# Fused layer-norm pieces, four weight slots and a routing-first passage to the experts, in a two-layer streaming step

## The chip, the cores and the metric

One core of a Trainium2 chip runs the whole program. The metric is the device time of one execution in microseconds (us): the kernel before takes 1603.79 us, the median of three runs (1601.14 to 1604.37). Engines are named as in the profile: PE is the matrix engine (TensorE), DVE is VectorE, ACT is ScalarE, POOL is GpSimd, and SP is the queue that issues most transfers (DMAs).

## The reference

288 tokens (256 of a prompt, 32 of a decode step) of width 1024 pass through two layers. In each layer:

```
z = x @ W_in                       # queries, keys, values, latents and two gates
m = W_out( sigmoid(ga) * Woa(FoX(x)) + sigmoid(gb) * Wob(MLA(x)) )
h = LN(alpha * x + m)
y = LN(alpha * h + FFN(h) + sigmoid(h W_pg) * (p W_pp))
```

FoX and MLA are two attention mixers. FFN is a dense SwiGLU of width 2816 in layer 0, and in layer 1 a mixture: a router picks the best 2 of 8 experts for each token, and each expert is a SwiGLU of width 2816. Everything is float32; besides y the new cache rows are returned.

## The kernel before, in words

**Layout.** Activations lie feature-major: 8 pieces of 128 features by 288 tokens. Weights come from memory in chunks of 128 x 1024 float32 (512 KB), each eight 128 x 128 tiles. Every product is made of three float32r matmuls: ACT copies a weight chunk, rounded, to `wh` (the high part) and `wl = raw - wh` (the low part) is subtracted on DVE and POOL; activations are split likewise into `xh` and `xl`. Lines 242 to 244 issue the three: xh·wh, xl·wh, xh·wl. The halves `wh` and `wl` have three slots of 1024 columns, given out in turn (`weight_slot`); a slot is free when the last matmul that reads it has run.

**Stages.** For each layer: "in" products and attention, gates and output products, a first layer norm (LN1), the feed-forward part, a second layer norm (LN2, in layer 0 inside the program, in layer 1 at its end). During LN1 PE has the eight small "pp" products (6 matmuls each; L643 moves each result from PSUM to `ple`), and behind them the eight "pg" products (24 matmuls each). These need all eight normalised pieces, since each piece is one step of the contraction. During LN2 of layer 0 PE has nothing but the "in" products of layer 1, which need the same; two of them end in a copy out of PSUM by DVE (`cq`, L402) that frees their PSUM buffers.

**A layer norm** (`norm_apply`, line 563). Two matmuls give mean `pm` and mean square `pv` over the features. ACT makes m2 (L597) and a copy mu (L598), DVE the variance (L599, L600), ACT the square root (L602), DVE the reciprocal (L608). Then a loop over the pieces c: DVE and POOL subtract mu (L577; piece 0 on DVE, the others on POOL), DVE multiplies by rstd (L616), ACT makes xh with gain and bias (L617), DVE (c < 5) or POOL makes x (L626), and DVE makes xl = x - xh (L629). Weight chunks of the products behind are split in between. All of it stands in a `manual_schedule` block, in which DVE, ACT and POOL keep the order that is written. PE, and everything outside such blocks, is ordered by the framework's planner from its own estimates. Each engine then runs its list strictly in that order.

**From LN1 of layer 1 to the experts** (the passage, L1266 to L1274). Three pg products, then the router (`route`: 24 small "lgp" matmuls, some forty small DVE operations, two "posp" matmuls), then `tokens` (transposes of x, copies to `xt` by DVE and ACT, three stores to a buffer `xd` in memory, L835), then slot lists (`slots`: one-hot matrices `dm` by DVE, L916, and "gsp" matmuls), then `fetch` (POOL gathers an expert's 128 token rows from `xd`, L928), then the remaining pg products, and `gather` (PE transposes the gathered rows, "gp", L939). The first expert product is "gu".

**Experts.** Eight experts in turn, each 66 half chunks of weights streamed through a ring (`mraw`) of 1 MB buffers, some 24 half chunks ahead; each half is split by ACT (L894), DVE (832 columns) and POOL (192, L896). "dn" is the product of an expert's second matrix.

## Time and profile before

| | before |
|---|---|
| median of three runs (lowest, highest) | 1603.79 us (1601.14, 1604.37) |
| the profiled execution, its time | 1602.14 us |
| the profiled execution, its span | 1600.4 us |
| PE / DVE / ACT / POOL busy | 95% / 74% / 62% / 53% |
| mean granted TensorE clock | 0.98 of full speed |

Times inside the trace are counted from the first instruction; the profiled execution's own time is 1.7 us longer than its span. A row of a timeline gives start, duration and, in brackets, how long the engine stood idle ahead of it and who ended that wait.

### The profile page before, as it was taken

How to read it: one execution, taken by the hardware profiler on the slowest of the kernel's cores; microseconds unless marked ns; L12 is line 12 of the kernel's file. 1: busy time of each engine (PE TensorE's matmuls, PEld its weight loads, DVE VectorE, ACT ScalarE, POOL GpSimd, SP SyncE). 2: the span in 40 equal slices, each digit the busy share in tenths (PEclk: the TensorE clock that was granted, in tenths of full speed). 3: DMA queues.
4: the chain of work that ended last, by engine and by line, in shares of the span. 5: the costliest groups of instructions: out<-in, count | busy, mean ns of one | idle time of the engine just before them, and what ended most of it. 6: DMA issues, size and time to landing. Idle time of an engine off the chain costs nothing. (4 is left out here: it accounts for less than half of the span.)

```text
span 1600.4 us, 25001 instructions
## 1 busy us (share of the span) xinstructions
PE 1526.9 (95%) x8930; PEld 1353.7 (85%) x8930; DVE 1178.0 (74%) x1567; ACT 993.1 (62%) x1417; POOL 850.3 (53%) x735
## 2 busy tenths in 40 slices
PE   6999998999997999998699999999999999999995
PEld 6999998999996999997587878878788787787874
DVE  6654667554458664578688888888888898888887
ACT  5454455444344464444487787877878778787784
POOL 5000132000016000245498887988879888898997
PEclk9999999999998999998899999999999999999998
DMA  7523444555553523883689999999999999999950
GB/s 213 181 65 105 154 133 145 163 167 163 167 166 111 174 80 93 275 298 106 235 333 361 351 362 350 361 360 343 372 347 366 357 352 357 346 360 347 349 188 32
DMA packets 85540, 391.61 MB, mean 245 GB/s; under 512 B 9728, under 2 KB 11648, under 8 KB 63776
## 3 DMA queue, kind: packets, MB, share of 16 engines
q1 hardware_dynamic: 83120, 382.76, 67.9%
q0 software_dynamic: 2224, 7.13, 1.4%
q8 instruction: 72, 1.18, 0.3%
q14 instruction: 60, 0.49, 0.1%
q10 hardware_dynamic: 64, 0.05, 0.0%
HBM read 384.75 MB, written 5.11 MB: 244 GB/s over the span
## 5 line engine op out<-in xcount | busy, mean ns | idle before, releaser
L896 POOL TENSOR_TENSOR wl<-mraw,wh 128x192 fp32r<-128x192 f32 x530 | 674.8, 1293 | 111.2 <-ACT wh L894 101.0
L896 DVE TENSOR_TENSOR wl<-mraw,wh 128x832 fp32r<-128x832 f32 x530 | 587.3, 1116 | 104.1 <-ACT wh L894 98.9
L894 ACT ACTIVATE wh<-mraw 128x1024 fp32r<-128x1024 f32 x530 | 556.3, 1057 | 133.3 <-PE dn L244 45.3
L227 DVE TENSOR_TENSOR wl<-raw,wh 128x1024 fp32r<-128x1024 f32 (+1 forms) x193 | 236.5, 1227 | 165.0 <-ACT wh L217 164.8
L217 ACT ACTIVATE wh<-raw 128x1024 fp32r<-128x1024 f32 (+1 forms) x196 | 199.3, 1020 | 241.5 <-PE mm L243 122.9
L242 PE MATMUL mm<-xh,wh 128*128 128x288 f32 x992 | 301.2, 305 | 22.3 <-DVE cq L402 7.7
L243 PE MATMUL mm<-xl,wh 128*128 128x288 f32 x992 | 301.6, 305 | 7.2 <-DVE xl L629 7.0
L244 PE MATMUL mm<-xh,wl 128*128 128x288 f32 x992 | 299.8, 303 | 0.3 <-DVE wl L227 0.2
L242 PE MATMUL gu<-wh,xg 128*128 128x512 f32 x704 | 283.2, 403 | 0.0
L243 PE MATMUL gu<-wl,xg 128*128 128x512 f32 x704 | 281.3, 400 | 1.0 <-DVE wl L896 0.9
L244 PE MATMUL gu<-wh,xg 128*128 128x512 f32 x704 | 277.9, 395 | 0.0
L242 PEld LDWEIGHTS mm<-xh,wh 128*128 128x128 f32 x992 | 192.4, 195 | 25.0 <-ACT xh L263 6.6
L243 PEld LDWEIGHTS mm<-xl,wh 128*128 128x128 f32 x992 | 191.3, 193 | 9.5 <-DVE xl L629 8.3
L244 PEld LDWEIGHTS mm<-xh,wl 128*128 128x128 f32 x992 | 191.2, 193 | 1.4 <-DVE wl L227 0.8
L243 PEld LDWEIGHTS gu<-wl,xg 128*128 128x128 f32 x704 | 132.8, 189 | 29.5 <-DVE wl L896 2.2
L242 PEld LDWEIGHTS gu<-wh,xg 128*128 128x128 f32 x704 | 132.5, 188 | 29.8 <-ACT xg L263 0.2
L244 PEld LDWEIGHTS gu<-wh,xg 128*128 128x128 f32 x704 | 132.3, 188 | 28.8 <-DVE xg L264 0.2
L243 PE MATMUL dn<-wl,hb 128*128 128x512 f32 (+1 forms) x374 | 144.3, 386 | 6.3 <-DVE wl L896 4.2
L244 PE MATMUL dn<-wh,hb 128*128 128x512 f32 (+1 forms) x374 | 142.6, 382 | 0.0
L242 PE MATMUL dn<-wh,hb 128*128 128x512 f32 (+1 forms) x374 | 142.6, 382 | 0.0
L550 POOL COPY s<-r 128x288 f32<-128x288 f32 x3 | 1.3, 425 | 178.4 <-DVE r L738 169.7
L243 PEld LDWEIGHTS dn<-wl,hb 128*128 128x128 f32 x374 | 70.2, 188 | 24.3 <-DVE wl L896 7.6
(343 smaller groups left out, 2142.2 us busy)
## 6 DMA issues: line engine op xcount, KB each, us to landing
mraw<-we SPq DMA_DIRECT2D x169, 1024.0 KB, 6.4
mraw<-we SPq DMA_DIRECT2D x192, 512.0 KB, 6.1
raw<-ws SPq DMA_DIRECT2D x187, 512.0 KB, 3.6
ok<-ka SPq DMA_DIRECT2D x2, 576.0 KB, 5.3
ov<-vf SPq DMA_DIRECT2D x4, 256.0 KB
xd<-xt SPq DMA_DIRECT2D x2, 512.0 KB, 3.2
x<-xT SPq DMA_DIRECT2D x3, 288.0 KB, 5.9
y<-ple SPq DMA_DIRECT2D x3, 288.0 KB, 2.1
```

Of the source, the lines that this page charges most:

```text
L217: self.nc.scalar.activation(wh[:, c:c + w], raw[:, c:c + w], AF.Copy)
L227: eng.tensor_tensor(wl[:, s], raw[:, s], wh[:, s].bitcast(F32), op=ALU.subtract)
L242: nc.tensor.matmul(ps, w[0], x[0], start=start, stop=False)
L243: nc.tensor.matmul(ps, w[0], x[1], start=False, stop=False)
L244: nc.tensor.matmul(ps, w[1], x[0], start=False, stop=stop)
L550: nc.gpsimd.tensor_copy(self.s1, rc)
L894: nc.scalar.activation(wh[:, c:c + w], src[:, c:c + w], AF.Copy)
L896: eng.tensor_tensor(wl[:, s], src[:, s], wh[:, s].bitcast(F32), op=ALU.subtract)
```

## The change

1. `norm_apply` is written anew. Per piece, DVE makes r·g·rstd in one operation (`scalar_tensor_tensor`), ACT adds the bias for xh, DVE makes xl = (t + b) - xh in one operation, and ACT makes x. So x moves from DVE and POOL to ACT. The subtraction of the mean reads `pm` in PSUM on DVE, except pieces 1 and 2, which stay on POOL. One pp product instead of two is evicted ahead of the square root; mu is copied behind it. The weight chunks of the next products are split before and during the norm at other places, by ACT and DVE alone.
2. Four weight slots instead of three. `qa`, `mh`, `ml` and others move into shared buffers.
3. In `linear` the three matmuls stand as xh·wh, xh·wl, xl·wh.
4. The passage is one hand-ordered block: logits and token transposes first, then pg0, routing, slot lists of experts 0 and 1 (index columns alone), their fetches, pg1 to pg7 with the gate values worked out between them. ACT does all `xt` copies and issues the stores to `xd`. The slot lists of experts 2 to 7 move into expert 0.

What moved, in three places. First ACT in LN1 of layer 0, before, from the square root (L602) on; `ple` rows evict pp products, `wh` rows split weight chunks:

```order
L602 ACTIVATE lrstd<-lrstd,eps 128x288 [waits DVE_49]
L604 ACT_TABLE_LOAD
L604 ACTIVATE warm<-mu 128x1 [waits Activation_49]
L643 ACTIVATE ple<-mm 128x288 [waits PE_49]
L217 ACTIVATE wh<-raw 128x1024 [waits DMAHW4_49]
L643 ACTIVATE ple<-mm 128x288 [waits PE_49] x2
L617 ACTIVATE xh<-r,vec 128x288 [waits DMASW2_49,DVE_49]
L643 ACTIVATE ple<-mm 128x288 [waits PE_49]
L217 ACTIVATE wh<-raw 128x1024 [waits DMAHW5_49]
L617 ACTIVATE xh<-r,vec 128x288 [waits DVE_49]
L643 ACTIVATE ple<-mm 128x288 [waits PE_49]
L617 ACTIVATE xh<-r,vec 128x288 [waits DVE_49]
```

and now (square root L610, `xh` L623, `x` L634, chunk splits L219):

```order
L610 ACTIVATE lrstd<-lrstd,eps 128x288 [waits DVE_49]
L611 ACTIVATE mu<-pm 128x288
L613 ACT_TABLE_LOAD
L613 ACTIVATE warm<-mu 128x1 [waits Activation_49]
L648 ACTIVATE ple<-mm 128x288
L648 ACTIVATE ple<-mm 128x288 [waits PE_49] x2
L219 ACTIVATE wh<-raw 128x512 [waits DMAHW7_49,PE_49]
L623 ACTIVATE xh<-r,vec 128x288 [waits DMASW2_49,DVE_49]
L648 ACTIVATE ple<-mm 128x288
L623 ACTIVATE xh<-r,vec 128x288 [waits DVE_49]
L648 ACTIVATE ple<-mm 128x288
L634 ACTIVATE x<-r,vec 128x288
```

One `ple` row fewer stands ahead of the table load, the first half of pg3's chunk, which waits for PE because its slot held pp weights, stands ahead of the first `xh`, and `x` rows have come to ACT.

Second, DVE in the same norm, two pieces of the loop, before:

```order
L616 TENSOR_TENSOR r<-r,lrstd 128x288 [waits Pool_49]
L626 TENSOR_SCALAR x<-r,vec 128x288 [waits DVE_49]
L629 TENSOR_TENSOR xl<-x,xh 128x288 [waits Activation_49]
L616 TENSOR_TENSOR r<-r,lrstd 128x288 [waits Pool_49]
L626 TENSOR_SCALAR x<-r,vec 128x288 [waits DVE_49]
L629 TENSOR_TENSOR xl<-x,xh 128x288 [waits Activation_49]
L227 TENSOR_TENSOR wl<-raw,wh 128x768 [waits DMAHW5_49]
```

and now (L622 is r·g·rstd, L584 the subtraction, L632 `xl`):

```order
L622 SCALAR_TENSOR_TENSOR r<-r,vec,lrstd 128x288 [waits Pool_49]
L584 TENSOR_TENSOR r<-r,pm 128x288
L632 SCALAR_TENSOR_TENSOR xl<-r,vec,xh 128x288 [waits Activation_49]
L622 SCALAR_TENSOR_TENSOR r<-r,vec,lrstd 128x288
L584 TENSOR_TENSOR r<-r,pm 128x288
L229 TENSOR_TENSOR wl<-raw,wh 128x512 [waits Activation_49]
L632 SCALAR_TENSOR_TENSOR xl<-r,vec,xh 128x288 [waits Activation_49]
```

Per piece DVE had three operations and now has three others, of which one is the subtraction that POOL made.

Third, PE around the gather of expert 0's rows, before (the last pg7 matmuls, then "gp", then "gu"):

```order
L243 MATMUL mm<-xl,wh 128x288
L244 MATMUL mm<-xh,wl 128x288
L939 MATMUL gp<-ident,xt 128x128 [waits DMASW4_49]
L939 MATMUL gp<-ident,xt 128x128 x7
L242 MATMUL gu<-wh,xg_7757 128x512 [waits Activation_49]
L243 MATMUL gu<-wl,xg_7757 128x512
L244 MATMUL gu<-wh,xg_7758 128x512 [waits DVE_49]
```

and now, inside pg4 and behind the index columns of expert 1:

```order
L255 MATMUL mm<-xh,wh 128x288
L256 MATMUL mm<-xh,wl 128x288
L257 MATMUL mm<-xl,wh 128x288
L940 MATMUL gsp<-gm,dm 128x2 [waits DVE_49,PE_49]
L940 MATMUL gsp<-gm,dm 128x2 [waits DVE_49] x2
L963 MATMUL gp<-ident,xt 128x128 [waits DMASW4_49,DVE_49,PE_49]
L963 MATMUL gp<-ident,xt 128x128 x3
L256 MATMUL mm<-xh,wl 128x288 [waits DVE_49]
L257 MATMUL mm<-xl,wh 128x288
```

The rows that fetch the gathered tokens stood behind all pg products; half of them now stands in the middle of pg4, and three and a half pg products are left behind it. The other half follows the gate columns, behind pg5:

```order
L256 MATMUL mm<-xh,wl 128x288
L257 MATMUL mm<-xl,wh 128x288
L940 MATMUL gsp<-gm,dm 128x2 [waits DVE_49]
L940 MATMUL gsp<-gm,dm 128x2 x5
L963 MATMUL gp<-ident,xt 128x128 x4
L255 MATMUL mm<-xh,wh 128x288 [waits Activation_49] x2
L256 MATMUL mm<-xh,wl 128x288 [waits DVE_49]
```

The diff:

```diff
     def weight_slot(self):
-        self.slot = (self.slot + 1) % 3
+        self.slot = (self.slot + 1) % 4
         s = slice(1024 * self.slot, 1024 * self.slot + 1024)
         return self.wh[:, s], self.wl[:, s]
 
-    def weight_hi(self, n, parts=1):
+    def weight_raw(self, n):
         raw = self.raw_tile(n % 3 == 2, "raw")
         self.nc.sync.dma_start(raw, self.i["ws"][n])
-        wh, wl = self.weight_slot()
+        return (raw, *self.weight_slot())
...
-        self.chunks = {k: v for k, v in self.chunks.items() if k > n - 3}
+        self.chunks = {k: v for k, v in self.chunks.items() if k > n - 4}
...
-            self.mm3(ps, self.weight(t + k), x, start and k == 0, stop and k == len(xs) - 1)
+            w, x = self.weight(t + k), x
+            nc = self.nc
+            nc.tensor.matmul(ps, w[0], x[0], start=start and k == 0, stop=False)
+            nc.tensor.matmul(ps, w[1], x[0], start=False, stop=False)
+            nc.tensor.matmul(ps, w[0], x[1], start=False, stop=stop and k == len(xs) - 1)
...
-    def norm_apply(self, l, off, r, last, head, ms, after):
+    def norm_apply(self, l, off, r, last, head, ms, mid=None, late=()):
...
-        after = list(after)
+        late = dict(late)
 
...
-        def sub(c, eng):
-            eng.tensor_tensor(r[:, c, :], r[:, c, :], mu, op=ALU.subtract)
-
-        pend = []
-
-        def hi():
-            if after:
-                n = after.pop(0) // CB
-                pend.append((n,) + self.weight_hi(n))
-
-        def lo(cut=CB * P):
-            if pend:
-                self.weight_lo(*pend.pop(0), cut=cut)
+        def sub(c):
+            eng, m = (nc.gpsimd, mu) if c in (1, 2) else (nc.vector, pm)
+            eng.tensor_tensor(r[:, c, :], r[:, c, :], m, op=ALU.subtract)
+
+        def half(c):
+            if mid is not None:
+                s = slice(c, c + 512)
+                nc.scalar.activation(wh[:, s], raw[:, s], AF.Copy)
+                return lambda: nc.vector.tensor_tensor(wl[:, s], raw[:, s], wh[:, s].bitcast(F32), op=ALU.subtract)
+            return lambda: None
 
         with self.tc.manual_schedule(engines={ENG.DVE, ENG.Activation, ENG.Pool}):
             last()
             c = KD - 1
+            if mid is not None:
+                raw, wh, wl = self.weight_raw(mid // CB)
+                self.chunks[mid // CB] = (wh, wl)
+            lo = [half(0)]
...
+            lo.pop()()
             nc.scalar.activation(m2, pm, AF.Square)
-            nc.scalar.activation(mu, pm, AF.Copy)
+            lo = [half(512)]
...
-            fill(2)
+            fill(1)
             nc.scalar.activation(rstd, rstd, AF.Sqrt, bias=self.eps[:, 0:1])
+            nc.scalar.activation(mu, pm, AF.Copy)
             if head is not None:
                 nc.scalar.activation(self.warm, mu[:, 0:1], AF.Tanh)
-            sub(0, nc.vector)
-            sub(1, nc.gpsimd)
-            sub(2, nc.gpsimd)
+            sub(0)
+            for c in (1, 2):
+                sub(c)
             nc.vector.reciprocal(rstd, rstd)
-            fill(1)
-            hi()
-            fill(2)
+            fill(3)
             for c in range(KD + 1):
                 if c < KD:
-                    g, b = self.col(l, off + c), self.col(l, off + 8 + c)
-                    t = r[:, c, :]
-                    nc.vector.tensor_tensor(t, t, rstd, op=ALU.mult)
-                    nc.scalar.activation(self.xh[:, c, :], t, AF.Identity, scale=g, bias=b)
+                    g, b, t = self.col(l, off + c), self.col(l, off + 8 + c), r[:, c, :]
+                    nc.vector.scalar_tensor_tensor(t, t, g, rstd, op0=ALU.mult, op1=ALU.mult)
+                    nc.scalar.activation(self.xh[:, c, :], t, AF.Identity, bias=b)
                     if c == 0:
-                        lo(512)
-                        for z in range(3, KD):
-                            sub(z, nc.gpsimd)
+                        lo.pop()()
                     fill(1)
-                    if c in (0, 4):
-                        hi()
-                    eng = nc.vector if c < 5 else nc.gpsimd
-                    eng.tensor_scalar(self.x[:, c, :], t, g, b, op0=ALU.mult, op1=ALU.add)
+                    if c + 3 < KD:
+                        sub(c + 3)
                 if c:
                     p = c - 1
-                    nc.vector.tensor_tensor(self.xl[p // 4][:, p % 4, :], self.x[:, p, :], self.xh[:, p, :].bitcast(F32), op=ALU.subtract)
-                if c in (3, 6):
-                    lo(768 if c == 3 else 1024)
+                    b, t = self.col(l, off + 8 + p), r[:, p, :]
+                    nc.vector.scalar_tensor_tensor(self.xl[p // 4][:, p % 4, :], t, b, self.xh[:, p, :].bitcast(F32),
+                                                   op0=ALU.add, op1=ALU.subtract)
+                    nc.scalar.activation(self.x[:, p, :], t, AF.Identity, bias=b)
+                if c in late:
+                    self.weight(late[c])
...
-            mg = self.pool(f"mg{l}", stack=sm)
-            mh = mg.tile([P, KD, T], F32R, name="mh")
-            ml = mg.tile([P, KD, T], F32R, name="ml")
+            mh = g.tile([P, KD, T], F32R, tag="A", name="mh")
+            ml = [g.tile([P, 4, T], F32R, tag=t, name="ml") for t in ("B1", "B2")]
...
+            t = [WHERE[(l, "pg"), m] for m in range(4)]
+            self.weight(t[0])
             self.ple = g.tile([P, KD, T], F32, tag="C", name="ple")
-            self.norm_apply(l, 0, r, evict, lambda m: self.pp(l, m), range(8), [WHERE[(l, "pg"), m] for m in range(3)])
+            self.xh = g.tile([P, KD, T], F32R, tag="A", name="xh")
+            self.xl = [g.tile([P, 4, T], F32R, tag=t, name="xl") for t in ("B1", "B2")]
+            self.norm_apply(l, 0, r, evict, lambda m: self.pp(l, m), range(8), t[1], {3: t[2], 7: t[3]} if l % 2 else {3: t[2]})
...
-            self.weight(t[0])
-            self.weight(t[1])
-            self.norm_apply(l, 16, r, evict, None, (), t[2:])
...
+            for x in t:
+                self.weight(x)
+            self.norm_apply(l, 16, r, evict, None, ())
...
+    def logits(self):
+        nc = self.nc
+        t = [self.ps_t.tile([P, 512], F32, tag="t", name="lgp") for z in range(2)]
+        self.lgp = [t[0][:, 0:NE], t[1][:, 0:NE], t[0][0:TS, NE:2 * NE]]
+        for bs in ((0, 1), (2,)):
+            for k in range(KD):
+                for b in bs:
+                    n = TS if b == 2 else P
+                    nc.tensor.matmul(self.lgp[b], self.x[:, k, b * P:b * P + n], self.wr[:, k, :], start=k == 0, stop=k == KD - 1)
+
+    def tokens(self):
+        nc, m1 = self.nc, self.m1
+        self.xd = self.dpool.tile([T, D], F32, name="xd")
+        xt = [m1.tile([P, D], F32, tag="xt", bufs=3, name="xt") for b in range(3)]
+        for z in range(2):
+            for b, n in enumerate((P, P, TS)):
+                pt = self.mps("tp", True)
+                for c in range(4):
+                    nc.tensor.transpose(pt[0:n, c * P:(c + 1) * P], self.x[:, 4 * z + c, b * P:b * P + n], self.ident)
+                nc.scalar.activation(xt[b][0:n, 512 * z:512 * z + 512], pt[0:n], AF.Copy)
+                if z:
+                    nc.scalar.dma_start(self.xd[b * P:b * P + n, :], xt[b][0:n])
+
+    def route(self, between):
...
+        for b in range(3):
+            for z in range(b + 1):
+                nc.tensor.matmul(ps[:, 8 * b:8 * b + 8], self.tri if z == b else self.ones, sel[:, z, :], start=z == 0, stop=z == b)
+        for b in range(3):
+            nc.tensor.matmul(ps[:, 32:40], self.ones, sel[:, b, :], start=b == 0, stop=b == 2)
+        self.cnt = ps[:, 32:40]
+        self.pos = m1.tile([P, 3, NE], F32, name="pos")
+        between()
+        nc.vector.scalar_tensor_tensor(self.pos, ps[:, 0:24].rearrange("p (b e) -> p b e", b=3), 1.0, sel, op0=ALU.add, op1=ALU.mult)
+
+    def gates(self):
...
-            if e + 2 < NE:
+            if 0 < e < NE - 2:
...
-                if e == 0 and g in (2, 5):
-                    self.slots((4, 5) if g == 2 else (6, 7))
+                if e == 0 and g in (1, 4, 7):
+                    self.slots((2 * (g // 3 + 1), 2 * (g // 3 + 1) + 1))
+                    if g == 1:
+                        self.fetch(2)
...
-        self.pgate(1, pgt, range(3), 6)
-        self.route()
-        self.tokens()
-        self.slots((0, 1))
-        self.fetch(0)
-        self.fetch(1)
-        self.cut = 512
-        self.pgate(1, pgt, range(3, 7), 6)
-        self.gather(0)
-        self.slots((2, 3))
-        self.pgate(1, pgt, range(7, 8), 6)
+        self.marks()
+        with self.tc.manual_schedule(engines={ENG.DVE, ENG.Activation, ENG.Pool}):
+            self.logits()
+            self.tokens()
+            ps = self.linear((1, "pg"), 0, self.xs())
+            n = WHERE[(1, "pg"), 4] // CB
+            raw, wh, wl = self.weight_raw(n)
+            self.chunks[n] = (wh, wl)
+            nc.scalar.activation(wh, raw, AF.Copy)
+
+            def low(c):
+                nc.vector.tensor_tensor(wl[:, c:c + 512], raw[:, c:c + 512], wh[:, c:c + 512].bitcast(F32), op=ALU.subtract)
+
+            self.route(lambda: low(0))
+            self.slots((0,), (2, 4))
+            self.fetch(0)
+            low(512)
+            self.slots((1,), (2, 4))
+            self.fetch(1)
+            gate(0, ps=ps)
+            gate(1)
+            self.weight(WHERE[(1, "pg"), 5])
+            gate(2)
+            self.gates()
+            gate(3)
+            self.slots((0, 1), (0, 2))
+            self.weight(WHERE[(1, "pg"), 6])
+            gate(4)
+            self.weight(WHERE[(1, "pg"), 7])
+            self.gather(0)
+            gate(5)
+            gate(6)
+            gate(7)
```

## Rows read from the trace of the kernel before

**Rows 1.** Windows by stage; the heading line names the columns, x the number of instructions

```profile
core 0: us, PE busy (x) PEld busy (x) DVE busy (x) ACT busy (x) POOL busy (x), PEclk, DMA share, GB/s
234.00:258.00 24.00, 17.63 (x102) 16.24 (x100) 20.63 (x32) 14.12 (x26) 12.57 (x12) 0.86 0.22 67
486.00:510.00 24.00, 13.42 (x78) 12.24 (x79) 21.41 (x37) 13.17 (x23) 15.91 (x15) 0.79 0.17 58
719.00:746.00 27.00, 22.05 (x152) 20.49 (x151) 21.67 (x35) 14.89 (x28) 13.89 (x14) 0.87 0.19 59
746.00:785.30 39.30, 24.10 (x168) 23.06 (x166) 28.41 (x85) 10.06 (x18) 20.85 (x23) 0.80 0.67 231
728.95:735.77 6.82, 5.81 (x24) 5.20 (x23) 6.30 (x14) 3.64 (x6) 2.75 (x4) 0.50 0.22 73
747.00:752.00 5.00, 5.00 (x40) 5.00 (x39) 4.75 (x11) 0.12 (x2) 4.74 (x5) 1.00 0.82 236
786.00:1570.00 784.00, 778.64 (x3538) 629.00 (x3537) 677.08 (x806) 617.59 (x737) 675.35 (x528) 1.00 0.91 339
```

**Rows 2.** Waits of TensorE: waiting line <- releaser: us in total, times, longest

```profile
PE gp L939 <- DMA xt<-xd,ati: 12.7, 1, 12.7
PE mm L243 <- DVE xl L629: 7.0, 6, 2.4
PE dn L243 <- DVE wl L896: 4.2, 9, 0.5
PE mm L242 <- ACT ple L643: 4.2, 3, 2.0
```

**Rows 3.** Timeline of VectorE, first layer norm of layer 0: start, us

```profile
233.70 0.46 DVE L599 TENSOR_TENSOR lrstd<-pv,m 128x288 f32<-128x288 f32 x1 [3.92 <-PE pv L596]
243.00 1.05 DVE L616 TENSOR_TENSOR r<-r,lrstd 128x288 f32<-128x288 f32 x1
247.75 0.45 DVE L616 TENSOR_TENSOR r<-r,lrstd 128x288 f32<-128x288 f32 x1
```

**Rows 4.** Timeline of GpSimd, same norm

```profile
240.11 4.60 POOL L577 TENSOR_TENSOR r<-r,mu 128x288 f32<-128x288 f32 x5
```

**Rows 5.** Timeline of ScalarE, same norm

```profile
234.99 0.54 ACT L602 ACTIVATE lrstd<-lrstd,eps 128x288 f32<-128x288 f32 x1 [1.24 <-DVE lrstd L600]
235.54 1.28 ACT L604 ACT_TABLE_LOAD   x1
241.32 0.63 ACT L617 ACTIVATE xh<-r,vec 128x288 fp32r<-128x288 f32 x1 [0.68 <-DVE r L616]
```

**Rows 6.** Timeline of TensorE, second layer norm of layer 0

```profile
493.60 1.09 PE L242 MATMUL mm<-xh,wh 128*128 128x288 f32 x3 [5.99 <-ACT xh L617]
497.11 0.61 PE L243 MATMUL mm<-xl,wh 128*128 128x288 f32 x1 [2.42 <-DVE xl L629]
509.76 0.37 PE L242 MATMUL mm<-xh,wh 128*128 128x288 f32 x1 [1.79 <-DVE cq L402]
```

**Rows 7.** Timeline of VectorE, second layer norm of layer 0

```profile
488.20 0.77 DVE L600 TENSOR_SCALAR lrstd<-lrstd 128x288 f32<-128x288 f32 x1
```

**Rows 8.** Timeline of TensorE, last router matmuls, gather and first expert product

```profile
744.64 1.11 PE L756 MATMUL lgp<-wr,x 128*128 128x8 f32 x20
783.52 1.97 PE L939 MATMUL gp<-ident,xt 128*128 128x128 f32 x8 [12.66 <-DMA xt<-xd,ati]
785.32 0.79 PE L242 MATMUL gu<-wh,xg 128*128 128x512 f32 x1
```

**Rows 9.** Timeline of VectorE, router and slot lists

```profile
750.54 0.18 DVE L766 TENSOR_REDUCE mx<-lg 128x3 f32<-128x24 f32 x1
750.75 0.18 DVE L768 TENSOR_TENSOR sel<-lg,mx 128x24 f32<-128x24 f32 x1
759.65 2.40 DVE L916 TENSOR_SCALAR dm<-iota,pos 128x128 fp32r<-128x128 f32 x6
```

**Rows 10.** The gather of token rows, its own view, all eight

```profile
DMA to landing us min/median/max: 3.9/5.9/9.1
```

More of the change, by code (lines that the diff above doesn't have):

```diff
@@ L67, in plan @@
             + [[(256 * j + 64, 64), (256 * j + 192, 64)] for j in range(4)])
-        lin((l, "gate"), "w_in", l, KD, [c for m in range(8) for c in
-            ([(GAOFF + m * P, P)], [(GBOFF + m * P, P)])])
+        lin((l, "gate"), "w_in", l, KD, runs(GAOFF, 8) + runs(GBOFF, 8))
         for m in range(8):
@@ L695, in phase @@
             r = g.tile([P, KD, T], F32, tag="D", name="r")
-            ms = self.pieces(mh, ml)
+            ms = [(mh[:, k, :], ml[k // 4][:, k % 4, :]) for k in range(KD)]
             self.pp_load(l)
@@ L800, in route @@
+        for b in range(3):
[5 more added lines that the diff above has]
+    def gates(self):
+        nc, m1 = self.nc, self.m1
+        mx1, s1, mx2, s2 = self.tops
         most = m1.tile([P, 1], F32, name="most")
-        nc.vector.tensor_reduce(most, cnt, axis=AX.X, op=ALU.max)
+        nc.vector.tensor_reduce(most, self.cnt, axis=AX.X, op=ALU.max)
```

135 lines of the change are left out of this document (57 added, 78 removed).

## The prediction

> **What bounds the kernel now.** I read the windows by stage first. Over the experts PE is busy 778.64 of 784 us at full clock [rows 1]: that half of the program is PE's, and only the 5.4 us in which it isn't busy can be won there. Around the layer norms and in the passage it is otherwise. From 486 to 510 PE is busy 13.42 of 24 us, and from 719 to the first expert product at 785.3 it is busy 22.05 + 24.10 = 46.15 of 66.3 us, with mean clocks of 0.79, 0.87 and 0.80 [rows 1]. So a change of norms and passage acts on the path, through two things: time in which PE stands, and time at half clock after it has stood (24 matmuls took 5.81 us in one half-clock stretch, 0.24 each, while 40 instructions, some of them short, took 5.00 in a full one [rows 1]; I count 0.13 for a 288-column matmul there). Second, PE's waits say on what: the gather 12.7 us once, `xl` 7.0 in six waits, `ple` 4.2, the experts' `wl` 4.2 in nine [rows 2]; the first `xh` of layer 0's second norm adds 5.99 [rows 6]. Third, the timelines of those places give the durations below.
>
> All sums are against the profiled execution, 1602.14 us, which lies 0.1% under the median of the runs, 1603.79; a difference worked out for the one is used for the other.
>
> **Pace of a piece.** A 128 x 288 operation on DVE takes 0.45 us at 247.75 and 1.05 at 243.00 [rows 3]; the slow one stands in the stretch in which POOL makes five subtractions in 4.60 us [rows 4]. The change takes all but two subtractions from POOL, all its x and all its chunk halves, so I price DVE's three operations of a piece at 3 x 0.45 = 1.35 us. The subtraction now reads PSUM: the row `lrstd<-pv,m` reads PSUM too and takes 0.46 [rows 3], so no surcharge. [...] ACT now has, per piece, xh and x. The old xh with gain and bias took 0.63; the square root, with a bias alone, 0.54 [rows 5]. So 2 x 0.54 = 1.08, plus a pp eviction of some 0.39 in LN1: 1.47 us. In LN1 ACT, not DVE, sets the pace; in LN2 DVE does.
>
> **LN2 of layer 0: -6.3 us.** The chain to the first xh loses the contended halves: 0.3 on the maximum (0.77 [rows 7]), 0.6 on r·rstd (1.05 to 0.45), 0.1 on xh, and some 0.3 because mu no longer stands ahead; PE restarts near 492.3 instead of 493.60 [rows 6]. The wait for the first xl, 2.42 [rows 6], shrinks to about one piece. Eight pieces at 1.35 end near 492 + 10.8 = 502.5 to 503; nine matmuls per piece fit in 1.2 us at full clock and trail in 2.2 at half, so the product ends between 503.5 and 505. With three finished chunks ahead of the norm and a fourth slot, the copy `cq` need not stand behind a chunk's halves, and PE goes on near 504.4 instead of 509.76 [rows 6]: 5.4. About half of the half-clock stretch that follows in the trace, some 0.9, goes too. Bounds: 4 if ACT's x pieces delay xh, 8 if nothing is left at half clock.
>
> **LN1 of layer 0: -0.7 us.** Here one gain and two losses meet. The pieces go at 1.47 instead of up to 2.7 us. But one eviction fewer stands ahead of the square root and the table load (0.54 and 1.28 [rows 5]), so PE runs dry one pp product (0.75 us) earlier, and its wait of 2.0 [rows 2] becomes 2.75. And a chunk split that needs a slot of the pp weights stands ahead of the first xh on ACT; it waits until PE has passed the middle pp products, and everything behind it on ACT waits too. Since the pg products still need 9.4 us of matmuls behind the first xh, little is left: between +0.5 and -2.
>
> **LN1 of layer 1 and the passage: -11.8 us.** Of the 46.15 us of work up to 785.3, 5.8 were done at half clock in the first window and about 5.2 in the second (0.20 x 2 x 39.3 = 15.7 us of half clock, less some 10.5 in which PE stood). At full clock that work would take half, so the floor is 46.15 - 5.5 = 40.7, and the first expert product could come at 759.7 at the earliest. What is left of stalls, in order: the pp wait, 2.75 as above. Then the gathered rows. The last router matmuls ran at 744.64 to 745.75 [rows 8], inside the pg products; now they stand right behind the last piece of x, near 736.5. Some twenty small DVE operations at 0.21 [rows 9] give 4.2, three one-hot columns at 0.4 (2.40 for six [rows 9]) with the gsp matmuls and casts about 4; the gather issues near 745 to 746 and takes its 1 us of POOL and 5.9 to land [rows 10]: 752 to 755. PE has pg0 to pg3 and a part of pg4 to fill in, about 4.3 x 24 x 0.13 = 13.5 us from 738 on, which ends near 752: a wait of 0 to 3, taken as 2.6. Behind it the gates: fourteen small operations on DVE at 0.2, behind three pieces of pg evictions, then six one-hots, then gsp: 2.9. The `wl` of pg6 stands behind that on DVE: 1.0. Together 9.3, and half-clock work after these waits, 4.5 (between the 3 of one stretch and the 6 of two). So 759.7 + 9.3 + 4.5 = 773.5 against 785.3 [rows 8]. Bounds: 16 if the waits of gather and gates are covered, 3 if the gather comes ten microseconds late.
>
> [...]
>
> **Experts, fourth slot: -4.3 us.** DVE's `wl` made PE wait 4.2 us in nine waits of at most 0.5 [rows 2], at the boundaries where DVE and ACT also split the next expert's activations. One more half chunk ahead (1.5 us of PE work) covers 0.5 us, and DVE, ACT and POOL, at 677, 618 and 675 busy of 784 [rows 1], can work ahead. All of the idle time is 5.4, the most; 2 if the slot only moves the wait.
>
> The order of the three matmuls and the moved buffers I cost at nothing: the split chunk is ready a slot ahead, and PE's work is the same. If that cover is missing the wait falls in the products' `wl`, some tenths. **Sum:** 6.3 + 0.7 + 11.8 + 4.3 = 23.1; 1602.1 - 23.1 = 1579.
>
> **The rivals.**
> - *The passage pays in new waits.* PE's order is fixed, and half of the gather now stands inside pg4 with 3.5 pg products behind it. If routing, stores and gather take ten microseconds longer than I count, PE stands ten longer. For it: before, 38 us lay from the last router matmul to the gather's first use. Against it: most of these went to slot lists of four experts and copies queued on DVE. The passage then gains 1.8: 1589.
> - *More than I count.* The waits of gather and gates (5.5 us) are covered, little is at half clock, LN2 gives 8 and the experts 5.4: 1569.
> - *The fourth slot gives nothing*, because POOL and DVE, each at 86% in the experts, set the pace there. For it: that share. Against it: the waits come at boundaries alone. 1583.
> - *Slower.* One mechanism: the gather inside pg4. Every microsecond by which the rows land after 755 is one of the whole program's, since PE can't go past it. The gain of all other parts is used up when they land 23 us late, near 778; that is about when they landed before (783.5), where nothing was queued behind. It needs the stores to `xd` (issued by ACT behind its copies) or the index columns to be held by a DVE or ACT operation that itself waits for PE. 1604 to 1612.
>
> **How the numbers follow.** My forecast 0.45, passage in new waits 0.21, more than counted 0.13, fourth slot idle 0.14, slower 0.07. A measurement of this kernel can tell 0.2% from no change (3.2 us). Only the slower case and the worst of the first rival come near: faster 0.90, same 0.04, slower 0.06. The range reaches from the third case's 1567 to 1593, past the passage case with the other lower bounds in part; outside lie about 0.17.
>
> **What would show it.** PE's wait in LN2 of layer 0 down from 5.99 to near 4.7, with xl pieces every 1.35 us; in both LN1 the wait for `ple` up to 2.75; the gather's wait from 12.7 to under 4 and no idle DVE behind the router; "gu" first at 770 to 777 less what came before (about 7); the 0.5 us waits at expert boundaries gone. Wrong it would be if PE stands over 8 us at "gp", if xl pieces in LN1 come slower than 2 us, or if the experts take longer than 784 us.

## The result, and the profile after

The changed kernel takes 1579.85 us, the median of four runs (1578.20 to 1579.97), against 1604.08 us for the kernel before on the same chip (1601.14 to 1604.72): a ratio of 0.985, with a 95% interval of 0.9833 to 0.9867. The forecast was 1579. The profiled execution took 1578.2 us with a span of 1576.3; TensorE is busy for 1522.3 us of it (97%), VectorE 1228.1, ScalarE 989.7, GpSimd 761.3.

First the windows by stage, of the kernel after, cut at its own places (columns as in [rows 1]): the first norm of layer 0, its second norm, the passage with the first norm of layer 1, the experts.

```profile
230.00:254.00 24.00, 19.33 (x116) 17.19 (x115) 16.71 (x32) 16.75 (x37) 2.91 (x3) 0.93 0.23 67
482.00:506.00 24.00, 16.87 (x106) 15.76 (x107) 20.48 (x42) 16.75 (x32) 9.97 (x12) 0.86 0.34 98
710.00:765.00 55.00, 47.03 (x334) 45.15 (x333) 38.35 (x111) 28.37 (x57) 8.75 (x8) 0.91 0.39 130
765.00:1556.00 791.00, 786.05 (x3610) 637.75 (x3608) 756.51 (x828) 610.37 (x744) 646.28 (x540) 1.00 0.91 340
```

Every stage around the norms has more busy TensorE and a higher clock than in [rows 1]: 16.87 us in the second norm's 24 at 0.86, where it was 13.42 at 0.79. In the experts 5.0 of 791 us are not busy. VectorE rose from 86% to 96% there (756.51 of 791) with the same work to do; the first experiment below says what raised it.

TensorE's waits after (columns as in [rows 2]), the longest and those that answer to [rows 2]:

```profile
PE mm L255 <- ACT xh L269: 5.9, 2, 4.7
PE mm L255 <- DVE cq L408: 5.5, 2, 4.6
PE mm L255 <- ACT ple L648: 5.5, 4, 2.5
PE mm L255 <- ACT xh L623: 5.3, 1, 5.3
PE mm L256 <- DVE wl L229: 3.3, 3, 1.6
PE gp L963 <- DMA xt<-xd,ati: 2.2, 1, 2.2
PE fst L1003 <- POOL finE L1010: 2.1, 1, 2.1
PE dn L245 <- DVE wl L915: 2.0, 5, 0.5
PE rmsp L328 <- ACT sq L327: 1.9, 1, 1.9
PE gu L245 <- DVE wl L915: 1.9, 4, 0.6
...
PE dn L245 <- POOL wl L915: 0.8, 1, 0.8
```

The gather's wait went from 12.7 to 2.2 us, the wait for `xl` (7.0 in six) is gone from the list, that of the experts' `dn` products for VectorE fell from 4.2 in nine to 2.0 in five while that of their `gu` products rose to 1.9, and that for `ple` rose from 4.2 to 5.5 with a longest of 2.5. Longer than before is `fst` at the end: 2.1 us for a sum on GpSimd.

Cut at six events that both traces have, the 24.0 us between the spans lie as follows (differences of start times, before and after; the last `dn` product and the span by their ends):

| stretch | before | after | change | forecast |
|---|---|---|---|---|
| start to the first `pp` product of layer 0 | 229.13 | 227.58 | -1.55 | 0 |
| to the means of its second norm (`pm`) | 257.25 | 254.47 | -2.78 | -0.7 |
| to the first `pp` product of layer 1 | 227.94 | 223.86 | -4.08 | -6.3 |
| to the first `gu` product | 71.00 | 58.95 (two early `gu` counted out) | -12.05 | -11.8 |
| to the last `dn` product | 795.45 | 791.11 (those counted in) | -4.34 | -4.3 |
| to the end of the span | 19.60 | 20.36 | +0.77 | 0 |

The hand order puts two `gu` products among the last `pg` ones, at 761.81 and 762.03; the cut between the fourth and the fifth stretch is moved by what they take.

### The profile page after: what moved, and what is told of

Its sections match the earlier page's. It is cut to its first block, busy times and chain, and to the rows that moved or that the text cites. A ratio compares the mean times of both kernels' runs of the same rounds, so it can differ in the third digit from the quotient of the medians.

```text
span 1576.3 us, 25018 instructions
## 1 busy us (share of the span) xinstructions
PE 1522.3 (97%) x8950; PEld 1353.1 (86%) x8950; DVE 1228.1 (78%) x1572; ACT 989.7 (63%) x1445; POOL 761.3 (48%) x689
## 3 DMA queue, kind: packets, MB, share of 16 engines
q10 hardware_dynamic: 400, 1.23, 0.2%
## 5 line engine op out<-in xcount | busy, mean ns | idle before, releaser
L915 POOL TENSOR_TENSOR wl<-mraw,wh 128x192 fp32r<-128x192 f32 x530 | 634.8, 1217 | 153.9 <-ACT wh L913 138.0
L915 DVE TENSOR_TENSOR wl<-mraw,wh 128x832 fp32r<-128x832 f32 x530 | 656.3, 1283 | 22.2 <-ACT wh L913 17.8
L913 ACT ACTIVATE wh<-mraw 128x1024 fp32r<-128x1024 f32 x530 | 543.7, 1054 | 93.4 <-PE dn L246 30.7
L229 DVE TENSOR_TENSOR wl<-raw,wh 128x1024 fp32r<-128x1024 f32 (+1 forms) x192 | 233.2, 1217 | 182.2 <-ACT wh L219 179.3
L257 PE MATMUL mm<-xl,wh 128*128 128x288 f32 x992 | 297.6, 302 | 0.0
L219 ACT ACTIVATE wh<-raw 128x1024 fp32r<-128x1024 f32 (+1 forms) x192 | 195.4, 1021 | 144.5 <-PE mm L257 105.8
```

The costliest lines, as they stand in the source:

```text
L219: self.nc.scalar.activation(wh[:, c:c + w], raw[:, c:c + w], AF.Copy)
L229: eng.tensor_tensor(wl[:, s], raw[:, s], wh[:, s].bitcast(F32), op=ALU.subtract)
L257: nc.tensor.matmul(ps, w[0], x[1], start=False, stop=stop and k == len(xs) - 1)
L913: nc.scalar.activation(wh[:, c:c + w], src[:, c:c + w], AF.Copy)
L915: eng.tensor_tensor(wl[:, s], src[:, s], wh[:, s].bitcast(F32), op=ALU.subtract)
```

## Experiments

Times are medians; ratios are to the kernel before on the same chip, with 95% intervals. "To `gu`" is the stretch from the first `pp` product of layer 1 to the first `gu` product, cut as in the table.

**Three slots in the experts alone.** The rotation goes by `nslot`, which is 4 until the first expert and 3 from there on.

```diff
-        self.slot = (self.slot + 1) % 4
+        self.slot = (self.slot + 1) % self.nslot
```

> The changed kernel, with the weight slots given out in a round of three instead of four from the first expert on; everything ahead of it as changed. Theory (the fourth slot covers the 0.5 us waits at expert boundaries): the stretch of the experts, 791.1 us from the first continuous gu to the last dn, goes back to about 795.4, the waits of dn and gu for DVE's wl from 3.9 us to about 5 or more with a wait of 0.48 at each boundary, and the time from 1579.9 to 1584. Rival (POOL and DVE set the pace in the experts and the slot gives nothing; the stretch is shorter for another reason, the earlier slot lists): no change, 1580.

Measured 1583.21 us, 0.9874 (0.9859 to 0.9890). From `gu` to the last `dn` it takes 796.2 us where the changed kernel takes 791.1, and its wait of the `dn` products is the one of [rows 2] again, to the tenth; the window's columns are those of [rows 1]:

```profile
PE dn L245 <- DVE wl L915: 4.2, 9, 0.5
PE dn L245 <- POOL wl L915: 2.0, 2, 1.3
...
765.00:1556.00 791.00, 783.53 (x3578) 634.04 (x3577) 687.05 (x825) 622.33 (x742) 679.83 (x534) 1.00 0.92 341
```

So the experts' term belongs to the fourth slot: 5.1 us by the stretch, which the second profile of the changed kernel (below) has at 791.1 too. The medians alone, with intervals that overlap, would not show it. TensorE's waits for split weights are 8.3 us in all here and 4.9 with four slots; these 3.4 are the waits' part of the 5.1. The slot also raised VectorE's share: in the same window VectorE is busy 687.05 us with three slots and 756.51 with four.

**The old order of the three products** (xh·wh, xl·wh, xh·wl).

```diff
-            nc.tensor.matmul(ps, w[1], x[0], start=False, stop=False)
-            nc.tensor.matmul(ps, w[0], x[1], start=False, stop=stop and k == len(xs) - 1)
+            nc.tensor.matmul(ps, w[0], x[1], start=False, stop=False)
+            nc.tensor.matmul(ps, w[1], x[0], start=False, stop=stop and k == len(xs) - 1)
```

> The changed kernel, with the three matmuls of a product in the order of before (xh times wh, then xl, then wl). Theory (costed at nothing): 1579.9 within 0.5, the first xl wait in a norm a little longer, the wl waits a little shorter. Rival (the order is what made the first layer norm of layer 0 gain 2.8 us instead of 0.7 and the start 1.5): 1581 to 1584, with waits for xl of 1 us and more back in the norms.

Measured 1585.23 us, 0.9887 (0.9871 to 0.9903). The interval lies above that of the changed kernel's first runs but overlaps that of its second runs below (0.9848 to 0.9881). What it lost in its trace lies in the first products of layer 1's attention, beside a stretch of 6.8 us at half clock (granted clock 0.50) that need not be its doing. Inconclusive: 5.4 us slower than the first runs, 2.1 than the second, and no cost proved. To the means of layer 0's second norm it needs 254.1 us, no more than the changed kernel.

**The old arithmetic of a piece**: subtraction on GpSimd, multiplication, gain and bias in ScalarE's xh, x by a vector operation, xl as x minus xh, and the copy of mu ahead of the root.

```diff
-            eng, m = (nc.gpsimd, mu) if c in (1, 2) else (nc.vector, pm)
+            eng, m = (nc.gpsimd if c else nc.vector), mu
...
-                    nc.vector.scalar_tensor_tensor(t, t, g, rstd, op0=ALU.mult, op1=ALU.mult)
-                    nc.scalar.activation(self.xh[:, c, :], t, AF.Identity, bias=b)
+                    nc.vector.tensor_tensor(t, t, rstd, op=ALU.mult)
+                    nc.scalar.activation(self.xh[:, c, :], t, AF.Identity, scale=g, bias=b)
```

> The changed kernel with the arithmetic of a norm piece as before: r times rstd on DVE, xh with gain and bias on ACT, x on DVE or POOL, xl from x, seven subtractions of mu on POOL, mu copied ahead of the square root; slots, early chunk halves and the passage as changed. Theory (POOL beside DVE made a piece 2.4 us): pieces slow again while POOL subtracts, the second norm of layer 0 gives back 3 to 4 us, the first norms 1 to 2 each; 1586 to 1588. Rival (the norms gained by the chunks split ahead of them, not by the pieces): 1580 to 1582.

Measured 1589.0 us, 0.9907 (0.9893 to 0.9920): some 9 us dearer than the first runs, 6 than the second. It is not where I had it: the first norm of layer 0 loses nothing (254.6 us to the means, against 254.47), layer 0's second norm 1.3, the passage 5.8 (64.7 to `gu`), and the end 2.4. The end is not the norm's doing: the second profile of the unchanged kernel, below, is 2.5 us longer there too. Nor is the router late by more than 0.6 us: its last matmul starts 27.1 us behind the first `pp` product, where it was 26.5. Most of the 5.8 lies at the gate columns, where TensorE waits 2.77 us until 761.59 for VectorE, and in half clock: 20.5 us of the passage instead of 10.2.

**The old passage order**: no order by hand; the planner places logits, routing, gates, tokens, gather and `pg`. The rest of the change stays, its `tokens()` too.

```diff
-        with self.tc.manual_schedule(engines={ENG.DVE, ENG.Activation, ENG.Pool}):
-            self.logits()
-            self.tokens()
...
+        for m in range(3):
+            gate(m, 6)
+        self.logits()
+        self.route(lambda: None)
+        self.gates()
+        self.tokens()
```

> The changed kernel with the passage in the order of before (pg0 to pg2, logits and routing, token copies, slot lists of experts 0 and 1 with gates, fetches, pg3 to pg6, gather, slot lists of 2 and 3, pg7) and left to the planner, not in a hand-ordered block; stores of tokens still issued by ACT, pos and gates in their new forms, all else as changed. Theory (the order of the passage gains 12 us): the gather's wait goes from 2.2 to about 12, the first gu comes 10 to 12 us later, 1590 to 1592. Rival (most of these 12 us come from the faster norm, the fourth slot and shorter routing operations): 1582 to 1585.

Measured 1578.71 us (1576.23 to 1580.16), 0.9842 (0.9827 to 0.9856): no slower than the changed kernel. To `gu` it takes 55.2 us, 3.8 less than with the hand order; it gives back 2.8 after the last `dn`, in a half-clock stretch of 6.8 us that the second profile of the changed kernel, below, has there too. My reason for half of the gain fell here.

**The kernel before, with the new `tokens()` alone**: each copy from the accumulator to `xt` by ScalarE instead of by ScalarE and VectorE in turn, stores issued by ScalarE instead of by SyncE, other accumulator banks, and the first halves of all three pieces ahead of the second ones.

```diff
-                self.copy(xt[0:n, 512 * z:512 * z + 512], pt[0:n])
-            nc.sync.dma_start(self.xd[b * P:b * P + n, :], xt[0:n])
+                nc.scalar.activation(xt[b][0:n, 512 * z:512 * z + 512], pt[0:n], AF.Copy)
+                if z:
+                    nc.scalar.dma_start(self.xd[b * P:b * P + n, :], xt[b][0:n])
```

> The kernel before with one function of the changed one: the token copies of the passage (all six copies to xt by ACT, their transposes in two other PSUM banks, the three stores to xd issued by ACT and not by SP behind the weight loads); order of the passage, routing, norms and slots as before. Theory, since the old order of the passage was as fast as the new one in the last runs (the third store, issued at 772.44, held the gather; copies on DVE and a queue full of weight loads held the store): the gather's wait goes from 12.7 to 3 to 5 us, the first gu comes 8 to 10 us earlier, 1594 to 1596. Rival (the gather then waits for the slot lists, which stand behind routing and the old norm on DVE): 1601 to 1604.

Measured 1598.22 us, 0.9971 (0.9961 to 0.9981). To `gu` it takes 62.65 us instead of 71.0, and the gather's wait fell from 12.7 to 4.1. The function alone takes 8 us out of the passage of a kernel that is otherwise unchanged; the profiled execution, the fastest of nine, is 6.7 us shorter, as the other stretches took 1.6 more; the ratio of all runs keeps 0.3%, some 5 us. The last token piece's transposes run at 751.83 there; its copy and store:

```profile
754.03 0.57 ACT L834 ACTIVATE xt<-tp 32x512 f32<-32x512 f32 x1
755.90 0.33 ACTq L836 DMA_DIRECT2D xd<-xt  x1
```

**The old passage order and the old `tokens()`**, on the changed kernel (the two diffs above, the second reversed).

> The changed kernel with the passage in the old order and, beyond that, the token copies of before (copies by DVE and ACT by turns, one kind of PSUM bank, stores issued by SP). Theory (copies and stores made the old passage slow): some 8 us over the old order alone, 1586 to 1588, with a gather wait of 10 us or more. Rival (norm and routing operations made it slow): 1579 to 1581.

Measured 1590.55 us, 0.9913 (0.9900 to 0.9927): 12 us behind the old order with the new function. The timeline shows why. SyncE's queue in this kernel (start, duration, DMA issued):

```profile
751.86 0.33 SPq L795 DMA_DIRECT2D xd<-xt  x1
...
755.37 0.33 SPq L795 DMA_DIRECT2D xd<-xt  x1
...
758.28 0.77 SPq L900 DMA_DIRECT2D mraw<-we  x1
759.18 0.62 SPq L795 DMA_DIRECT2D xd<-xt  x1
```

The same kernel on VectorE, GpSimd and TensorE:

```profile
758.25 0.67 DVE L281 COPY xt<-tp 32x512 f32<-32x512 f32 x1
...
767.53 1.08 POOL L951 DMA_INDIRECT xt<-xd,ati  x1 [7.44 <-DMA xd<-xt]
...
772.27 1.97 PE L962 MATMUL gp<-ident,xt 128*128 128x128 f32 x8 [14.31 <-DMA xt<-xd,ati]
```

The last token piece waits for a copy on VectorE (758.25 to 758.92), its store leaves SyncE's queue 0.3 us later (759.18), behind a load of expert weights, the gather waits 7.44 us for the store to land, and TensorE 14.31 for the gather. In the kernel before, the same chain stood later:

```profile
768.66 0.60 PE L833 MATMUL tp<-ident,x 128*32 128x128 f32 x4
771.74 0.67 DVE L275 COPY xt<-tp 32x512 f32<-32x512 f32 x1
772.44 0.33 SPq L835 DMA_DIRECT2D xd<-xt  x1
777.68 1.09 POOL L928 DMA_INDIRECT xt<-xd,ati  x1 [4.98 <-DMA xd<-xt]
```

With the old order and the new function the last store leaves ScalarE's queue at 744.37, and the gather waits for an index instead:

```profile
743.77 0.57 ACT L794 ACTIVATE xt<-tp 32x512 f32<-32x512 f32 x1
744.37 0.33 ACTq L796 DMA_DIRECT2D xd<-xt  x1
...
754.71 1.17 POOL L952 DMA_INDIRECT xt<-xd,ati  x1 [0.44 <-DVE gsv L947]
...
761.36 1.94 PE L963 MATMUL gp<-ident,xt 128*128 128x128 f32 x8 [4.36 <-DMA xt<-xd,ati]
```

**The early chunk of layer 0's first norm at the end of the loop**, as in layer 1.

```diff
-  range(8), t[1], {3: t[2], 7: t[3]} if l % 2 else {3: t[2]})
+  range(8), t[1], {3: t[2], 7: t[3]})
```

> The changed kernel with pg3's chunk of layer 0 split at the end of the norm's loop, as in layer 1, so that none of its halves stands ahead of the first xh on ACT. Theory (that half waited 2.7 us for a slot and held the first xh, which was computable at 236.7 and came at 239.5): the two waits in this norm behind 244 us (1.25 us) and the one at 239.9 go, 1.0 to 1.7 us faster than the changed kernel: 1578.2 to 1578.9. Rival (PE had pp matmuls left until 239.9 anyway and the pieces are held by the chunk of pg2 on DVE): no change, 1579.9.

Measured 1580.71 us, 0.9864 (0.9849 to 0.9879). The three waits of 0.47, 0.39 and 0.86 us behind the chunk's halves became one of 0.63 at 243.5 and one of 1.43 at 250.55: moved, not gone.

**The sum of squares of the last two pieces on VectorE**, at the end of the program.

```diff
-            nc.gpsimd.tensor_tensor(self.s2, self.s2, q, op=ALU.add)
+            (nc.vector if c > 3 else nc.gpsimd).tensor_tensor(self.s2, self.s2, q, op=ALU.add)
```

> The changed kernel with two of the ten sums of the last norm's statistics (the squares of pieces 4 and 5) on DVE and not on POOL. Theory (after the last dn PE waited 2.14 us for POOL's chain of sums): the wait falls under 1 us and the end comes 1.2 to 2 us earlier, 1578 to 1578.7. Rival (DVE's own chain takes its place, since the last scaled rows wait on DVE too): no change, 1579.9.

Measured 1579.88 us, 0.9852 (0.9837 to 0.9867); the wait at `fst` fell from 2.14 to 1.62. The other sum, still on GpSimd, held it.

**The changed kernel again**, as the measure for the three that follow.

> The changed kernel once more, unchanged, beside the next three on one chip. It should give 1580 within 1.5; a difference of the next kernels is read against this run.

Measured 1583.12 us (1580.41 to 1584.6), 0.9865 (0.9848 to 0.9881). This is outside the 1.5 us that I allowed. The waits are those of the first profile, but in layer 0's second norm it has 10.2 us at half clock instead of 6.8, and 6.8 us more behind the last `dn`, where the stretch to the end takes 22.9 us instead of 20.4. Its four runs have a mean granted clock of 0.984 to 0.988, the longest the lowest; the first four had 0.988 and 0.989. So the medians of an unchanged kernel lie some 3 us apart, and the two profiled executions 6.4 (1578.2 and 1584.6); smaller differences between two sets of runs say nothing.

**Three slots throughout.** A slot is handed out here while a later product still names its chunk, so some products use other weights.

> The changed kernel with three weight slots throughout. Theory (the fourth slot gives 4 to 5 us in the experts, and the chunk halves split ahead of the norms, which need it, are what gained 2.8 us in the first norm of layer 0): the experts' stretch back to about 796, from the first pp product to the second norm's mean 256.5 to 257 instead of 254.5, about as much in layer 1; 1587 to 1590. Rival (only the experts need the fourth slot): 1583 to 1584, as with three slots in the experts alone.

Measured 1613.24 us, 1.0056; it makes two more raw loads of weights than the changed kernel (189, not 187). That spoils it as an answer on the norms. Waits of 0.48 us came back at the expert boundaries, as with three slots in the experts alone.

**The old passage order, and both sums of the last two pieces on VectorE**; then **the same with two products instead of one ahead of the square root** in the norms.

```diff
-            nc.gpsimd.tensor_tensor(self.s1, self.acc[:, 0, :] if c == 1 else self.s1, a, op=ALU.add)
-            nc.gpsimd.tensor_tensor(self.s2, self.s2, q, op=ALU.add)
+            eng = nc.vector if c > 3 else nc.gpsimd
+            eng.tensor_tensor(self.s1, self.acc[:, 0, :] if c == 1 else self.s1, a, op=ALU.add)
+            eng.tensor_tensor(self.s2, self.s2, q, op=ALU.add)
... and in the second kernel:
-            fill(1)
+            fill(2)
...
-            fill(3)
+            fill(2)
```

> The changed kernel with the passage in the old order, left to the planner, and with all four sums of the last two summed pieces of the last norm on DVE. Theory (the old order with ACT's token copies brings the first gu 3.8 us nearer to the pp products; POOL's chain of sums then holds PE for 2.14 us, after which it can fall to half clock): the wait of fst for POOL falls under 0.7 us, 1575 to 1577. Rival (the end waits for DVE just as long): 1578 to 1579, as with the old order alone.

> The kernel before this one with two pp results, and not one, moved out of PSUM ahead of the square root, as in the kernel before the change. Theory (PE's wait for the pp results, 2.46 us in both first norms, is 0.75 longer for the one eviction fewer): the wait falls to 1.7 to 2.0 in both, the norms' pieces start 0.4 later; 0.5 to 1 us faster than the kernel before it. Rival (the later square root costs as much): no change to it.

Measured 1575.63 us, 0.9827 (0.9813 to 0.9841), and 1572.44 us (1571.88 to 1574.29), 0.9807 (0.9794 to 0.9820). The second is faster than the kernel before and the changed one; its interval doesn't touch that of the changed kernel measured beside it (0.9848 to 0.9881). Its waits of TensorE:

```profile
PE mm L255 <- ACT ple L648: 5.6, 4, 1.9
...
PE gp L963 <- DMA xt<-xd,ati: 4.3, 1, 4.3
...
PE fst L1003 <- DVE finE L1011: 0.8, 1, 0.8
```

The first wait for `ple` in the two first norms is 1.66 and 1.67 us, not 2.46 and 2.35, but in layer 0 the next one is 1.94 instead of 0.47, so the total is no smaller. `fst` waits 0.8 instead of 2.1. Between the two kernels the intervals overlap (0.9794 to 0.9820 and 0.9813 to 0.9841), and 1.8 of the 2.5 us between the profiled spans lie in the passage, where the waits are alike (6.6 us) and the half clock is not: that the second `pp` eviction gained is not shown.

## Why the prediction was right, and where its steps were not

**The experts: right in size, with the slot as the cause, but by the forecast's waits only in half.** -4.34 measured, -4.3 forecast, and taking the slot away in the experts alone gives it back (5.1 us). The forecast had the 4.2 us of waits for VectorE's `wl` covered. Before, two more groups stood beside them:

```profile
PE dn L243 <- POOL wl L896: 2.0, 2, 1.3
PE gu L243 <- DVE wl L896: 0.9, 2, 0.6
```

That makes 7.1 us, and 4.9 are left: of seven waits of 0.48 us at the boundaries five are gone, and those at 1326.10 and 1425.92 stayed. So 2.2 of the 4.3 us stand in waits; the rest stands in no wait of the trace, and that the sum met the forecast is in part luck. The bound "5.4, the most" came from a window that ended at 1570: the 2.0 us of waits for GpSimd lie behind it. For the same reason the experts' 791.1 us can't be held against the 784 among the signs of being wrong. The rival "the fourth slot gives nothing" fell with the first experiment. The share that spoke for it rose to 96% on VectorE, and it was the slot that raised it; the stretch became shorter all the same.

**The passage: right in size, wrong in cause.** -12.05 against -11.8, but the forecast came from the routing at the front ("now they stand right behind the last piece of x"), with the gather inside `pg4`. With the old order the stretch is 3.8 us shorter still. What the step left out is in the rows of the fences above: in the kernel before, the chain that set the gather was not the router but the third token piece. Its transposes ran at 768.66, its copy was VectorE's at 771.74, behind the work queued there, and the gather waited 4.98 us for its store. SyncE's queue did not hold that store: it left at 772.44, 0.03 us behind the copy's end, while on ScalarE, with the new function alone, it left 1.3 us behind it (755.90). From issue to landing, too, the queue makes no difference to be seen: 3.2 to 7.5 us for the stores on SyncE's queue whose landing a trace has, 2.3 to 8.0 on ScalarE's. What came earlier there are the transposes (768.66 to 751.83) and the copy (771.74 to 754.03). The function changes their order, their banks, the copying engine and the issuing queue at once; which of the first three did it, no run shows. I named the "copies queued on DVE" against a rival, and never priced what earlier copies would give, although [rows 8] gave me the end of the chain and the timelines its links.

The new function takes 8 us out of the passage of the kernel before, some 5 out of the whole; going back to the old one costs 12 in the changed kernel with the old order. The faster norm may be the passage's second part (5.8 us when it is undone, most of it at the gates and in half clock). These sizes overlap and don't add up: each measures what is late next. The hand order together with the old function was not run; so the order may have been another way to the same gain, but beside the new function it adds none. By TensorE's waits the account closes: between the first `pp` product of layer 1 and the first `gu` they sum to 20.2 us before and to 8.0 after.

The sizes within it came closer. The gather and the gates after, TensorE and GpSimd:

```profile
743.89 1.05 POOL L952 DMA_INDIRECT xt<-xd,ati  x1 [30.04 <-DVE wl L1297]
...
748.72 0.63 PE L963 MATMUL gp<-ident,xt 128*128 128x128 f32 x4 [2.20 <-DMA xt<-xd,ati]
750.91 0.41 PE L256 MATMUL mm<-xh,wl 128*128 128x288 f32 x1 [1.57 <-DVE wl L229]
...
761.81 0.39 PE L244 MATMUL gu<-wh,xg 128*128 128x512 f32 x1
```

The wait of 2.20 answers to the 2.6 forecast and to 12.66 in [rows 8]; the gather issues at 743.89, where 745 to 746 was forecast. Of the gates' 2.9 nothing is seen, they are covered; the waits for split chunks are 1.57, 0.41 and 0.84 where 1.0 stood in the sum. VectorE was not without idle time behind the router, as one sign had it: it stands 4.04 us until 742.88 for a slot-list product of TensorE. The stores that rival four needed to be late leave ScalarE's queue at 733.82, 734.85 and 735.87, eight microseconds and more ahead of the gather, and the rows land in time: the slower case fell.

On the gather beside a busy VectorE: from its issue at 743.89 to the product that uses it at 748.72 pass 4.8 us, and the view of all eight gathers after says

```profile
DMA to landing us min/median/max: 4.4/7.8/10.1
```

against 3.9/5.9/9.1 in [rows 10]. Six of the eight run beside the experts, where VectorE is at 96%, and no product waited for one of them; the one on the path lies at the short end, landing 4.7 us behind its issue. That VectorE's share sets the landing is not shown: the median is 1.9 us longer than before, but with three slots in the experts, and VectorE less busy (687.05 us against 756.51), it is 7.8 us too, 7.2 with three slots throughout, and 7.1 in the second profile of the changed kernel.

**The second norm of layer 0: right in kind, mis-sized**, -4.08 against -6.3. VectorE after, from the limit on the variance on:

```profile
483.89 0.31 DVE L608 TENSOR_SCALAR lrstd<-lrstd 128x288 f32<-128x288 f32 x1
485.10 0.46 DVE L584 TENSOR_TENSOR r<-r,pm 128x288 f32<-128x288 f32 x1 [0.90 <-ACT mu L611]
485.47 1.95 DVE L617 RECIPROCAL lrstd<-lrstd 128x288 f32<-128x288 f32 x1
487.45 0.52 DVE L622 SCALAR_TENSOR_TENSOR r<-r,vec,lrstd 128x288 f32<-128x288 f32 x1
487.89 0.45 DVE L584 TENSOR_TENSOR r<-r,pm 128x288 f32<-128x288 f32 x1
...
489.05 0.51 DVE L632 SCALAR_TENSOR_TENSOR xl<-r,vec,xh 128x288 fp32r<-128x288 f32 x1
...
490.27 0.51 DVE L632 SCALAR_TENSOR_TENSOR xl<-r,vec,xh 128x288 fp32r<-128x288 f32 x1
```

ScalarE beside it, and TensorE's restart:

```profile
484.24 0.53 ACT L610 ACTIVATE lrstd<-lrstd,eps 128x288 f32<-128x288 f32 x1 [0.93 <-DVE lrstd L608]
484.68 0.39 ACT L611 ACTIVATE mu<-pm 128x288 f32<-128x288 f32 x1
...
488.59 0.61 PE L255 MATMUL mm<-xh,wh 128*128 128x288 f32 x1 [5.29 <-ACT xh L623]
```

The limit takes 0.31 with GpSimd idle instead of the 0.77 of [rows 7], when GpSimd subtracted beside it (488.01 to 489.61), as forecast. But the "0.3 because mu no longer stands ahead" turned round: the subtraction that stands ahead of the reciprocal on VectorE is released by the copy of mu at 485.10, so the reciprocal begins at 485.47, some 0.7 us after the root was there. The restart waits 5.29 us where 4.7 was forecast. The pieces then came at 1.22 us, not 1.35, the `xl` wait of 2.42 [rows 6] is gone, and TensorE is at half clock for 6.8 us instead of 13.7, which is better than forecast. Behind the norm the gain stayed out: the 1.79 us at `cq` [rows 6], which the forecast had gone, is 0.95 there and 0.85 at `t`, and `rmsp` waits 1.92 us at 514.65, where it waited 1.09 before. The missing 2.2 us are those plus the mu copy, as far as the rows tell; no run takes them apart.

**The first norm of layer 0: wrong in size**, -2.78 against -0.7. The wait for `ple` grew to 2.46, close to the 2.75 forecast, and the chunk split ahead of the first xh cost what it should:

```profile
238.93 0.63 ACT L219 ACTIVATE wh<-raw 128x512 fp32r<-128x512 f32 x1 [2.69 <-PE mm L257]
239.47 0.52 ACT L623 ACTIVATE xh<-r,vec 128x288 fp32r<-128x288 f32 x1
```

Both losses are there and the stretch is still shorter. What went is in the trace: before, TensorE waited 1.43, 1.76 and 0.54 us for `xl` behind the first `xh`, and it was at half clock for 6.8 us; after, it waits 0.47, 0.39 and 0.86 us there, and half clock is 3.4 us. The forecast priced the faster pieces at next to nothing, and the half clock in this norm at nothing. Which edit did it is open: neither the arithmetic of a piece (254.6 us without it), nor the order of the products (254.1), nor the early chunk makes the difference alone.

**What wasn't forecast.** The start's 1.55 us need be no more than chance: variants of the changed kernel with the same instructions there reach the first `pp` product between 227.4 and 229.4, and the kernel before at 229.1. The end's +0.77 is a cost of the change. TensorE's `fst` after:

```profile
1558.12 0.75 PE L1003 MATMUL fst<-finE,meanw 128*128 128x288 f32 x2 [2.14 <-POOL finE L1010]
```

It waited 0.68 us there before, and 0.69 with three slots in the experts alone: the wait came with the fourth slot. With all four sums on VectorE the wait is 0.77, and the stretch to the end 18.6 us instead of 20.4.

So the total was right to 0.1% because the two large terms were right in size and the errors of the small ones (-2.1, +2.2, -1.5, +0.8) nearly cancel; the last is luck. One slip of the prediction changes nothing: the lower end of its range, 1567, is called the third case's, which says 1569.

## What to carry to other kernels

When TensorE waits for a DMA, follow the chain back over every link of it, transposes, copy, store and landing, and compare the end of each link with the start of the next: here the store left its queue 0.03 us behind its copy, so the late copy and not the queue held the gather. After a rewrite, try each part undone: here the longest part of the diff (the order by hand) added nothing to a short function inside it, which had the gain. A copy moved off the chain must be followed to whoever reads it, or it comes back one engine further on.

## What was not expected of the hardware

- A fused operation with two tensors and a column on VectorE, 128 x 288 in f32, takes 0.51 to 0.52 us, against 0.45 for a plain one; the subtraction that reads its mean from the accumulator (`r<-r,pm`) takes 0.443 to 0.455 us in all eighteen of its rows, so no surcharge was seen; the same subtraction on GpSimd takes 0.79 in all six of its rows, where five in a row took 4.60 before [rows 4], 0.92 each.
- VectorE's subtraction of an expert's `wl`, 128 x 832, takes 1.29 us in the mean with four weight slots and 1.12 with three slots in the experts (from 800 to 1540 us of each trace), at the same work; GpSimd's, 128 x 192, takes 1.23 and 1.30. No run shows why.
- The same kernel had 6.8 us at half clock in layer 0's second norm in one profile and 10.2 in another, with the same waits ahead of it, and 6.8 us more at the end in the second; its medians were 1579.85 and 1583.12 us.
